# Batch normalisation on one core: a short transfer before every store, and loads issued after 4000 columns

## The chip, the cores and the metric

The kernel runs on one core of a Trainium2 chip. The time is the device time of one execution in microseconds (us); the time before is the median of three runs. Beside it there is one profiled execution with its trace, from which all durations are taken. Engines are named as in the profile: DVE is VectorE, ACT is ScalarE, SP is SyncE; the DMA engines are the sixteen that move data between memory (HBM) and the on-chip buffers (SBUF) for this core.

## The reference

An inference batch normalisation of a 32 x 256 x 128 x 128 float32 tensor, with one mean, variance, factor and offset per channel:

```python
def reference(x, gamma, beta, running_mean, running_var):
    eps = 1e-5
    mean = running_mean.reshape(1, -1, 1, 1)
    ...
    return gamma * (x - mean) / np.sqrt(var + eps) + beta
```

The kernel computes it as `x * scale + shift`, with `scale = gamma / sqrt(var + eps)` and `shift = beta - mean * scale` for each channel. The tensor is 536.87 MB; it is read once and written once.

## The kernel before

**Tiles.** `xr` and `outr` view the tensor as 64 tiles (NT): 32 images by two blocks of 128 channels. A tile has 128 partitions (channels) of 16,384 columns, that is 128 rows of 65,536 bytes, 8.39 MB. Three buffers `bufs[0..2]` hold one tile each; tile i uses buffer i mod 3, is computed in place and stored from there. [...]

**Head** (lines 90 to 128). SP issues the left half of tile 0, then four loads of parameters (L93), each of which puts the same 1024 bytes into 16 rows, then the right half (L97) and tiles 1 and 2 (L99). VectorE and ScalarE turn the parameters into `scale_t` and `shift_t`.

**VectorE** (L155 to L158) takes the left columns of each tile in two instructions at L132: columns 0 to VFIRST (2560), which counts the semaphore `vfirst`, then VFIRST to VMOST (14,336), which counts `vdone`. The last tile goes to VLAST (9216), the first to VHEAD (8192) in one instruction.

**ScalarE** (L166 to L173) takes the other columns with one activation at L143 (2048 columns of most tiles), which counts `adone`, waits for `vdone`, and issues the store of the tile (L171) on its own queue. Before the activation, for tiles 1 to 61, it waits at L168 for `gone(i - 1)`: all of the store of the tile before has been written. So at most one store is in flight for most of the run.

**SP** (L161 to L164) issues the load of tile i when the store of tile i - 3, which used the same buffer, is gone, and when `vfirst` has reached i - 1: VectorE has done the first 2560 columns of tile i - 1, so that tile has landed. So at most one load is in flight too after the head. At the end SP waits for the last three stores (L177).

A DMA of a whole tile gives each of the sixteen DMA engines eight rows of 65,536 bytes and, behind them, a packet of 4 bytes that counts the semaphore. Loads issued by SP are on queue q1, stores issued by ScalarE on queue q10; each DMA engine serves both.

Of the kernel before, what the change touches and what calls it, by code (L numbers as in the profile page):

```python
# [8 lines left out]
NBUF = 3  # L9
PAD = 936  # L10
NHEAD = 3
VFIRST = 2560
VMOST = 14336
VHEAD = 8192
VLAST = 9216


@with_exitstack
def kernel(
    ctx: ExitStack,  # L20
    tc: tile.TileContext,
    x: bass.AP,
    gamma: bass.AP,
    beta: bass.AP,
    running_mean: bass.AP,
    running_var: bass.AP,
    out: bass.AP,
):
    nc = tc.nc
    eps = 1e-5  # L30
    f32 = mybir.dt.float32

    N, C, H, W = x.shape
    P = nc.NUM_PARTITIONS
    assert C % P == 0
    NCB = C // P
    HW = H * W
    NT = N * NCB
    B = 32
    NQ = P // B  # L40
    NE = 16
    NPAR = 4

    xr = x.rearrange("n (cb p) h w -> (n cb) p (h w)", p=P)
    outr = out.rearrange("n (cb p) h w -> (n cb) p (h w)", p=P)

    params = ctx.enter_context(tc.tile_pool(name="params", bufs=1))
    data = ctx.enter_context(tc.tile_pool(name="data", bufs=1))
    params.tile([P, PAD], f32, name="pad", tag="pad")
    bufs = [data.tile([P, HW], f32, name=f"t{s}", tag=f"t{s}") for s in range(NBUF)]  # L50
    rows = params.tile([B, NPAR * C], f32, name="rows", tag="rows")
    turned = params.tile([B, NPAR * C], f32, name="turned", tag="turned")
    par = params.tile([P, NPAR, NCB], f32, name="par", tag="par")
    eps_t = params.tile([P, 1], f32, name="eps_t", tag="eps")
    std_t = params.tile([P, NCB], f32, name="std_t", tag="std")
    rstd_t = params.tile([P, NCB], f32, name="rstd_t", tag="rstd")
    scale_t = params.tile([P, NCB], f32, name="scale_t", tag="scale")
    ms_t = params.tile([P, NCB], f32, name="ms_t", tag="ms")
    shift_t = params.tile([P, NCB], f32, name="shift_t", tag="shift")

    loaded = [tc.alloc_semaphore(f"loaded{s}") for s in range(NBUF)]
    stored = [tc.alloc_semaphore(f"stored{s}") for s in range(NBUF)]
    early = tc.alloc_semaphore("early")
    first = [tc.alloc_semaphore(f"first{s}") for s in range(NHEAD)]
    vfirst = tc.alloc_semaphore("vfirst")
    vdone = tc.alloc_semaphore("vdone")
    adone = tc.alloc_semaphore("adone")
    fetched = tc.alloc_semaphore("fetched")  # L70
    vec = tc.alloc_semaphore("vec")
    act = tc.alloc_semaphore("act")

    with tc.tile_critical():  # L74
        count = [0]

        def step(inst, sem=None, value=None):
            if sem is not None:
                inst._wait_ge(sem, value)
            elif count[0]:  # L80
                inst._wait_ge(vec, count[0])
            inst.then_inc(vec, 1)
            count[0] += 1
            return count[0]

        left, right = slice(0, HW // 2), slice(HW // 2, HW)
        last = NT - 1


        nc.sync.dma_start(out=bufs[0][:, left], in_=xr[0][:, left]).then_inc(early, 16)  # L90
        zeroed = step(nc.vector.memset(rows[:], 0.0))  # L91
        for r, ap in enumerate((running_var, gamma, beta, running_mean)):
            inst = nc.sync.dma_start(out=rows[0:NE, r * C : (r + 1) * C], in_=ap.partition_broadcast(NE))  # L93
            if r == 0:
                inst._wait_ge(vec, zeroed)
            inst.then_inc(fetched, 16)
        nc.sync.dma_start(out=bufs[0][:, right], in_=xr[0][:, right]).then_inc(first[0], 16)  # L97
        for i in range(1, NHEAD):
            nc.sync.dma_start(out=bufs[i][:], in_=xr[i]).then_inc(first[i], 16)  # L99

        def landed(i):
            if i < NHEAD:
                return first[i], 16
            s = i % NBUF
            before = 1 if s < NHEAD else 0
            return loaded[s], 16 * (i // NBUF + 1 - before)


        step(nc.vector.memset(eps_t[:], eps))  # L109
        step(nc.vector.transpose(out=turned[:], in_=rows[:]), fetched, 16 * NPAR)  # L110
        blocks = turned.rearrange("p (rc q b) -> p rc q b", q=NQ, b=B)
        flat = par.rearrange("p r cb -> p (r cb)")
        for q in range(NQ):
            placed = step(nc.vector.tensor_copy(out=flat[q * B : (q + 1) * B], in_=blocks[:, :, q, 0]))  # L114
        var_t, gamma_t, beta_t, mean_t = (par[:, r] for r in range(NPAR))
        nc.scalar.activation(  # L116
            out=std_t[:],
            in_=var_t,
            func=mybir.ActivationFunctionType.Sqrt,
            bias=eps_t[:],  # L120
            scale=1.0,
        )._wait_ge(vec, placed).then_inc(act, 1)
        step(nc.vector.reciprocal(out=rstd_t[:], in_=std_t[:]), act, 1)  # L123
        step(nc.vector.tensor_mul(out=scale_t[:], in0=gamma_t, in1=rstd_t[:]))  # L124
        step(nc.vector.tensor_mul(out=ms_t[:], in0=mean_t, in1=scale_t[:]))  # L125
        ready = step(nc.vector.tensor_sub(out=shift_t[:], in0=beta_t, in1=ms_t[:]))  # L126
        nc.vector.wait_ge(vec, ready)
        nc.scalar.wait_ge(vec, ready)

        def vector_part(i, first_col, end):  # L130
            t, cb = bufs[i % NBUF], i % NCB
            return nc.vector.tensor_scalar(  # L132
                out=t[:, first_col:end],
                in0=t[:, first_col:end],
                scalar1=scale_t[:, cb : cb + 1],
                scalar2=shift_t[:, cb : cb + 1],
                op0=mybir.AluOpType.mult,
                op1=mybir.AluOpType.add,
            )

        def scalar_part(i, first_col):
            t, cb = bufs[i % NBUF], i % NCB
            return nc.scalar.activation(  # L143
                out=t[:, first_col:],
                in_=t[:, first_col:],
                func=mybir.ActivationFunctionType.Identity,
                bias=shift_t[:, cb : cb + 1],
                scale=scale_t[:, cb : cb + 1],
            ).then_inc(adone, 1)

        def gone(i):
            return stored[i % NBUF], 16 * (i // NBUF + 1)


        vector_part(0, 0, VHEAD)._wait_ge(early, 16).then_inc(vdone, 1)  # L155
        for i in range(1, NT):
            vector_part(i, 0, VFIRST)._wait_ge(*landed(i)).then_inc(vfirst, 1)
            vector_part(i, VFIRST, VLAST if i == last else VMOST).then_inc(vdone, 1)  # L158


        for i in range(NHEAD, NT):  # L161
            s = i % NBUF
            nc.sync.wait_ge(*gone(i - NBUF))
            nc.sync.dma_start(out=bufs[s][:], in_=xr[i])._wait_ge(vfirst, i - 1).then_inc(loaded[s], 16)  # L164

        for i in range(NT):  # L166
            if 0 < i < NT - 2:
                nc.scalar.wait_ge(*gone(i - 1))  # L168
            scalar_part(i, VHEAD if i == 0 else VLAST if i == last else VMOST)._wait_ge(*landed(i))
            nc.scalar.wait_ge(vdone, i + 1)  # L170
            nc.scalar.dma_start(out=outr[i], in_=bufs[i % NBUF][:])._wait_ge(adone, i + 1).then_inc(  # L171
                stored[i % NBUF], 16
            )  # L173


        for i in range(NT - NBUF, NT):
            nc.sync.wait_ge(*gone(i))  # L177

# [29 lines left out]
```

## Time and profile before

| | us |
|---|---|
| time, median of 3 runs | 2486.29 (2485.91 to 2487.04) |
| the profiled execution, its own time | 2487.21 |
| its span, first to last instruction | 2485.4 |
| VectorE busy | 505.3 (20%) |
| ScalarE busy | 144.9 (6%) |
| load, issue to landing, median | 37.0 |
| store, issue to landing, median | 36.5 |

How to read the profile: the span is what one execution took from its first to its last instruction; the time of the execution holds a little more. The page gives the busy share of each engine and of the DMA engines in 40 equal slices, the DMA queues with the share of the sixteen engines' span that their packets took, the chain of work that ended last, followed back from the end, and groups of instructions with their mean duration. A timeline line has start and length in us, engine, line of the code, operation, and in brackets how long the engine stood idle before it and what released it; a length that covers several instructions ("x2") runs from the first's start to the last's end. The trace also holds a record of each DMA packet: queue, bytes, start and duration.

VectorE waited for landing loads for 1938.7 us in total, ScalarE for stores to be gone for 2243.3 us, SP for stores for 1693.3 us and for VectorE's first columns for 689.5 us.

### The profile page before, as it was taken

The page shows a single profiled execution, that of the slowest core. Times are in us where ns is not written, and L with a number is a line of the kernel's source. Part 1 is how long each engine was busy: PE and PEld are TensorE (multiplying, and loading weights), DVE is VectorE, ACT ScalarE, POOL GpSimd, SP SyncE. Part 2 cuts the span into 40 slices and gives each one's busy share as a digit, 9 for nine tenths or more (in the row PEclk, how much of TensorE's full clock was granted, in tenths as well). Part 3 has the DMA queues.
Part 4 walks back from the last instruction along what each step waited for, and adds up shares of the span by engine and source line. Part 5 has one row for each costly group of instructions (what it writes and reads, how often), then busy time and mean ns, then how long its engine had stood idle before and what let it go on. Part 6 is the DMA issues. An engine that isn't in the chain of part 4 may idle for free.

```text
span 2485.4 us, 578 instructions
## 1 busy us (share of the span) xinstructions
DVE 505.3 (20%) x138; ACT 144.9 (6%) x66; POOL 0.2 (0%) x4
## 2 busy tenths in 40 slices
DVE  2122121221212212122121121211212212122120
ACT  1000000000000000000000000000000000000001
POOL 0000000000000000000000000000000000000000
DMA  9999999999999999999999999999999999999999
GB/s 421 424 439 438 422 439 433 428 438 436 426 438 437 425 438 437 428 436 436 437 427 437 436 427 438 431 429 439 423 438 437 433 429 436 437 428 437 435 428 405
DMA packets 18708, 1073.85 MB, mean 432 GB/s; under 512 B 2128, under 2 KB 2192, under 8 KB 2192
## 3 DMA queue, kind: packets, MB, share of 16 engines
q1 hardware_dynamic: 9488, 536.94, 50.0%
q10 hardware_dynamic: 9216, 536.88, 49.9%
q14 instruction: 4, 0.03, 0.0%
HBM read 536.94 MB, written 536.87 MB: 432 GB/s over the span
## 4 chain that ended last, share of the span: by engine, by line
DMA 93%; DVE 4%; another core or an unknown queue 1%; ACT 0%; issue 0%; SPq 0%; DVEq 0%
DMA t<-in_x_dram 93%; DVE t L132 4%; ACT t L143 0%; SPq L93 0%; DVE rows L91 0%; SPq L97 0%; DVE eps_t L109 0%; DVEq L203 0%; SPq L74 0%
## 5 line engine op out<-in xcount | busy, mean ns | idle before, releaser
L132 DVE TENSOR_SCALAR t<-t,scale_t,shift_t 128x11776 f32<-128x11776 f32 (+2 forms) x127 | 501.8, 3993 | 1938.8 <-DMA t<-in_x_dram 1938.7
L143 ACT ACTIVATE t<-t,shift_t,scale_t 128x2048 f32<-128x2048 f32 (+1 forms) x64 | 143.3, 2239 | 2299.2 <-DMA out_dram<-t 2243.3
L110 DVE STREAM_TRANSPOSE turned<-rows 32x1024 f32<-32x1024 f32 x1 | 1.2, 1232 | 12.0 <-DMA rows<-in_running_mean_dram 12.0
L116 ACT ACT_TABLE_LOAD x1 | 1.3, 1283 | 0.9 <-SPq L74 0.9
L91 DVE MEMSET rows<- 32x1024 f32 x1 | 0.9, 912 | 1.2 <-SPq L74 1.2
L116 ACT ACTIVATE std_t<-par,eps_t 128x2 f32<-128x2 f32 x1 | 0.3, 295 | 14.1 <-DVE par L114 14.1
L114 DVE COPY par<-turned 32x8 f32<-32x8 f32 x4 | 0.6, 162 | 0.1
L123 DVE RECIPROCAL rstd_t<-std_t 128x2 f32<-128x2 f32 x1 | 0.2, 165 | 0.4 <-ACT std_t L116 0.4
L125 DVE TENSOR_TENSOR ms_t<-par,scale_t 128x2 f32<-128x2 f32 x1 | 0.2, 161 | 0.0
L126 DVE TENSOR_TENSOR shift_t<-par,ms_t 128x2 f32<-128x2 f32 x1 | 0.2, 161 | 0.0
L124 DVE TENSOR_TENSOR scale_t<-par,rstd_t 128x2 f32<-128x2 f32 x1 | 0.2, 160 | 0.0
L192 POOL MEMSET const-bfloat16-1.0<- 128x1 bf16 x1 | 0.1, 101 | 0.0
L192 POOL MEMSET const-uint8-127<- 128x1 uint8 x1 | 0.1, 101 | 0.0
L192 POOL MEMSET const-float32-0.0<- 128x1 f32 x1 | 0.1, 98 | 0.2 <-issue 0.2
L192 POOL MEMSET const-float32-1.0<- 128x1 f32 x1 | 0.1, 98 | 0.0
L109 DVE MEMSET eps_t<- 128x1 f32 x1 | 0.1, 59 | 0.1
## 6 DMA issues: line engine op xcount, KB each, us to landing
t<-in_x_dram SPq DMA_DIRECT2D x2, 4096.0 KB, 15.9
out_dram<-t ACTq DMA_DIRECT2D x64, 36.5
t<-in_x_dram SPq DMA_DIRECT2D x63, 37.0
rows<-in_running_var_dram SPq DMA_DIRECT2D x1, 16.0 KB, 11.2
rows<-in_gamma_dram SPq DMA_DIRECT2D x1, 16.0 KB, 11.1
rows<-in_beta_dram SPq DMA_DIRECT2D x1, 16.0 KB, 10.8
rows<-in_running_mean_dram SPq DMA_DIRECT2D x1, 16.0 KB, 10.7
```

The costliest lines, as they stand in the source:

```text
L91: zeroed = step(nc.vector.memset(rows[:], 0.0))
L109: step(nc.vector.memset(eps_t[:], eps))
L110: step(nc.vector.transpose(out=turned[:], in_=rows[:]), fetched, 16 * NPAR)
L114: placed = step(nc.vector.tensor_copy(out=flat[q * B : (q + 1) * B], in_=blocks[:, :, q, 0]))
L116: nc.scalar.activation(out=std_t[:], in_=var_t, func=mybir.ActivationFunctionType.Sqrt, bias=eps_t[:], scale=1.0,)._wait_ge(vec, placed).t ...
L123: step(nc.vector.reciprocal(out=rstd_t[:], in_=std_t[:]), act, 1)
L124: step(nc.vector.tensor_mul(out=scale_t[:], in0=gamma_t, in1=rstd_t[:]))
L125: step(nc.vector.tensor_mul(out=ms_t[:], in0=mean_t, in1=scale_t[:]))
L126: ready = step(nc.vector.tensor_sub(out=shift_t[:], in0=beta_t, in1=ms_t[:]))
L132: return nc.vector.tensor_scalar(out=t[:, first_col:end], in0=t[:, first_col:end], scalar1=scale_t[:, cb : cb + 1], scalar2=shift_t[:, cb ...
L143: return nc.scalar.activation(out=t[:, first_col:], in_=t[:, first_col:], func=mybir.ActivationFunctionType.Identity, bias=shift_t[:, cb : ...
L192: nc = _bacc.Bacc("TRN2", target_bir_lowering=False, num_devices=1)
```

## The change

For tiles 1 to 61 ScalarE's part becomes two activations: 640 columns (STEP), which count a new semaphore `begun`, and the remaining 2048, which count `adone` as before. Between them it issues a small transfer of its own queue: eight rows (HALF) of 16 float32, 64 bytes each, all from the first 16 values of `gamma` into the first 16 columns of eight partitions of `pad`, which nothing reads. Its issue waits for `begun`, so for the end of the 640 columns, and, from tile 2 on, for the small transfer of the tile before (`aside`). Then come the 2048 columns, the wait for `vdone`, and the store. VMOST goes from 14,336 to 13,696, so that VectorE gives up the 640 columns, and VFIRST from 2560 to 4000: the load that waits for `vfirst` waits for 4000 columns of VectorE. At the end SP waits for the last small transfer too.

```diff
-VFIRST = 2560
-VMOST = 14336
+VFIRST = 4000
+VMOST = 13696
+STEP = 640
+HALF = 8
...
-        def scalar_part(i, first_col):
+        def scalar_part(i, first_col, end, done):
             t, cb = bufs[i % NBUF], i % NCB
             return nc.scalar.activation(
-                out=t[:, first_col:],
-                in_=t[:, first_col:],
+                out=t[:, first_col:end],
+                in_=t[:, first_col:end],
...
-            ).then_inc(adone, 1)
+            ).then_inc(done, 1)
...
         for i in range(NT):
+            first_col = VHEAD if i == 0 else VLAST if i == last else VMOST
             if 0 < i < NT - 2:
                 nc.scalar.wait_ge(*gone(i - 1))
-            scalar_part(i, VHEAD if i == 0 else VLAST if i == last else VMOST)._wait_ge(*landed(i))
+                scalar_part(i, first_col, first_col + STEP, begun)._wait_ge(*landed(i))
+                first_col += STEP
+                if i > 1:
+                    nc.scalar.wait_ge(aside, 16 * (i - 1))
+                nc.scalar.dma_start(
+                    out=pad[0:HALF, 0:16], in_=gamma[0:16].partition_broadcast(HALF)
+                )._wait_ge(begun, i).then_inc(aside, 16)
+            scalar_part(i, first_col, HW, adone)._wait_ge(*landed(i))
             nc.scalar.wait_ge(vdone, i + 1)
             nc.scalar.dma_start(out=outr[i], in_=bufs[i % NBUF][:])._wait_ge(adone, i + 1).then_inc(
                 stored[i % NBUF], 16
             )
 
 
+        nc.sync.wait_ge(aside, 16 * (NT - 3))
         for i in range(NT - NBUF, NT):
             nc.sync.wait_ge(*gone(i))
```

## The prediction

> **What bounds the kernel now.** I read the page's slices of the span and its queues first, then its chain, then the chain in order of time and the timeline of a middle stretch, then the groups by shape.
>
> ```profile
> DMA  9999999999999999999999999999999999999999
> q1 hardware_dynamic: 9488, 536.94, 50.0%
> q10 hardware_dynamic: 9216, 536.88, 49.9%
> DMA 93%; DVE 4%; another core or an unknown queue 1%; ACT 0%; issue 0%; SPq 0%; DVEq 0%
> ```
>
> The sixteen DMA engines have work in every slice; the packets of the load queue (q1) and the store queue (q10) fill 99.9% of sixteen engines' span. The chain says "93% loads", but that is not where time could be won: while a load is on the chain the engines also carry the store.
>
> ```profile
> 435.99 36.96 DMA t<-in_x_dram
> 472.95 0.02 issue
> 472.98 1.62 DVE t L132
> 474.60 0.02 issue
> 474.62 36.97 DMA t<-in_x_dram
> ...
> 400.00:2400.00 2000.00, 408.34 (x103) 107.23 (x52) 0.00 (x0) 1.00 1.00 433
> ```
>
> Columns above: start and length in us of a piece of the chain; the last line is a window of 2000 us (busy DVE, ACT, POOL, clock, DMA share, GB/s). One tile takes 474.62 - 435.99 = 38.63 us. A tile is 128 rows of 65,536 bytes in and as many out, so each engine has 8 + 8 rows to move: 38.63 / 16 = 2.414 us a row. The trace's packet records say the same directly: of 16,256 packets of 65,536 bytes, loads and stores alike, about 98% took 2418 ns (the next starts 4 ns before the end), and none under 2410. That holds whether the other engines are loading or storing at that moment. So an engine has its own rate and no idle time: the 1032 data packets of an engine (16 of them half as long) are 2471.9 us; the first starts 2.0 us into the span and the last ends 1.7 us before its end; what is over is 9.8 us on the last engine, 3.7 (loads) and 2.4 (stores) of it, on the mean of the engines, by packets that took longer. **The whole gain to be had is 9.8 us (0.4%); any nanosecond added to the packets of an engine that is behind is added to the time.**
>
> Why no engine runs dry is the second thing to read:
>
> ```profile
> 657.35 2.09 ACT L143 ACTIVATE t<-t,shift_t,scale_t 128x2048 f32<-128x2048 f32 x1 [37.32 <-DMA out_dram<-t]
> 659.47 0.34 ACTq L171 DMA_DIRECT2D out_dram<-t  x1
> 666.98 7.93 DVE L132 TENSOR_SCALAR t<-t,scale_t,shift_t 128x2560 f32<-128x2560 f32 x2 [31.50 <-DMA t<-in_x_dram]
> 668.62 0.33 SPq L164 DMA_DIRECT2D t<-in_x_dram  x1
> 695.96 2.09 ACT L143 ACTIVATE t<-t,shift_t,scale_t 128x2048 f32<-128x2048 f32 x1 [36.52 <-DMA out_dram<-t]
> 698.08 0.34 ACTq L171 DMA_DIRECT2D out_dram<-t  x1
> ```
>
> One load and one store are in flight. A load's end releases VectorE, and 1.64 us later the next load is issued; a store's end releases ScalarE, and 2.12 us later the next store is issued. By the packet records an engine's cycle is: four store rows alone (the load is being turned round), four pairs, four load rows alone (the store is being turned round). Four rows are 9.66 us of cover for each turnaround.
>
> **The change part by part.** Durations come from the groups by shape:
>
> ```profile
> L132 DVE TENSOR_SCALAR t<-t,scale_t,shift_t 128x11776 f32<-128x11776 f32 x62 | 397.2, 6407 | 0.0
> L143 ACT ACTIVATE t<-t,shift_t,scale_t 128x2048 f32<-128x2048 f32 x62 | 129.8, 2093 | 2250.8 <-DMA out_dram<-t 2243.3 <-DMA t<-in_x_dram 7.5
> L132 DVE TENSOR_SCALAR t<-t,scale_t,shift_t 128x2560 f32<-128x2560 f32 x63 | 101.6, 1612 | 1938.7 <-DMA t<-in_x_dram 1938.7
> L143 ACT ACTIVATE t<-t,shift_t,scale_t 128x7168 f32<-128x7168 f32 x1 | 6.4, 6361 | 41.5 <-DMA t<-in_x_dram 41.5
> ```
>
> 1. Loads follow 4000 columns. VectorE: (6407 - 1612) / (11776 - 2560) = 0.520 ns a column, so 1612 + 1440 x 0.520 = 2361 ns: the load is issued 0.75 us later. Its second piece has 9696 columns, about 5.3 us; the store waits for it, but VectorE ends some 21 us before ScalarE starts that tile (666.98 + 7.93 against 695.96). The load's first packets start 3.4 to 5.2 us after issue while stores run, and four more store rows stand behind them, so nothing runs dry: some engines do a fifth store row alone. Cost 0; without that cover 61 x 0.75 = 46 us.
>
> 2. ScalarE's part is 2688 columns in two instructions, and a DMA issue between. Slope (6361 - 2093) / (7168 - 2048) = 0.834 ns a column, so 640 columns take 2093 - 1408 x 0.834 = 0.92 us; the issue 0.34 (the row at L171), steps between 0.03 to 0.05. The store is issued about 1.35 us later (0.92 + 0.34 + 0.09). Behind it on ScalarE nothing waits but the next tile. On the engine that is furthest behind the first store packet of line 659.47 starts 4.58 us after issue, as its loads last that long; 3.23 us would be left. From issue to a first packet takes 1.01 us on an idle engine (the span's first load, issued at 0.95) and at most 2.42 us (the smallest seen here without a gap). So that engine stays fed, with 0.8 to 2.2 us to spare. Engines ahead may stand still up to about 1 us and then are less ahead, which costs nothing at the end. Cost 0; without that cover 61 x 1.35 = 82 us.
>
> 3. The wait for the short transfer before (`aside`) was satisfied a tile earlier, the last wait on SP lies under the last stores: 0. No queue of POOL is passed. The added ScalarE instructions, transfers and waits make the program about 40% longer; there were four fetches of 8192 bytes on q14 in mid-run, two more at 0.4 to 0.7 us on one engine each: 0.5 us taken.
>
> 4. **The short rows themselves.** 61 transfers of 8 rows of 64 bytes, each a packet and a 4-byte count on one engine, between two long packets. This isn't in the trace. Nearest rows from both sides: below, a 4-byte packet takes 9 ns and shifts the next by 6, a row of 1024 bytes takes 46; so 0.016 us and, were it to smooth what follows, less than nothing (a rival below). Above, a short packet lets too little be fetched behind it: after the four q14 packets of 8192 bytes (309 ns) the next 65,536 bytes took 2528, 2542, 2569 and 2768 ns, that is 110, 124, 151 and 350 too many; the three small ones are those with a 4-byte packet between. And the four 16-row parameter loads in the head, one row per engine each:
>
> ```profile
> 10.00:12.00 2.00, 0.00 (x0) 0.00 (x0) 0.00 (x0) 1.00 0.99 426
> 12.00:13.00 1.00, 0.00 (x0) 0.00 (x0) 0.00 (x0) 1.00 1.39 455
> 13.00:14.00 1.00, 0.00 (x0) 0.00 (x0) 0.00 (x0) 1.00 0.58 234
> 14.00:16.00 2.00, 1.67 (x4) 0.00 (x0) 0.00 (x0) 1.00 1.10 475
> 16.00:18.00 2.00, 1.39 (x7) 0.29 (x1) 0.00 (x0) 1.00 1.06 459
> 18.00:20.00 2.00, 2.00 (x1) 0.00 (x0) 0.00 (x0) 1.00 0.80 344
> ```
>
> These ten us moved 409 GB/s on the mean, against 433 in mid-run: 0.54 us lost, 0.14 a row. The packet records agree: mostly 0.48 us from the last long packet's end to where the next would have begun, and that next took about 1500 ns where 1213 is usual. I take the mean of the three q14 rows, 0.128, and 0.016 for the packets: 0.144 us a tile, as a single foreign packet amid long ones is nearest to it. 61 x 0.144 = 8.8 us on eight engines, which nothing hides as they are never idle. The ends kept for the range are 0 and 0.66 us (309 - 4 + 350, if the whole slot of the slowest q14 case is a fetch delay that 8192 bytes only covered): 0 to 40 us.
>
> [...]
>
> **Sum.** 8.8 + 0.5 = 9.3 us. The profiled execution took 2487.21 us, 1.8 more than its span of 2485.4, and is 0.9 over the median of 2486.29. The median plus 9.3 is 2495.6.
>
> **The rivals.**
> - *The short row is nearly free* (0.016 to 0.06 us): 1 to 4 us, 2487 to 2490, no change that can be told; a measurement of this kernel tells 0.2%, 5 us, from none. For it: counts between long packets shift them by 6 ns, so what is fetched ahead reaches past a tiny packet. Against it: q14 and the head. Not slower; it decides if the fetch ahead spans two packets. 0.33.
> - *The whole delay is paid*: 0.45 to 0.66 us a tile, 2514 to 2527. For it: both q14 and the head come to 0.43 to 0.66 us for a slot of any size. Against: in the head rows followed each other at 48 ns. 0.08.
> - *The engines run dry at each store.* If the store gets in after the slowest engine's loads have ended, the load's count is not held back by a store packet; the next load then comes after three store rows (0.37 + 2.36 + 0.05 + about 3.5 = 6.3 us, under 7.24), so only three load rows cover the store: 2.41 + 0.54 + 3.48 + (1.01 to 2.42) - 7.24 = 0.2 to 1.6 us idle per tile, which keeps itself up. 12 to 98 us, 2498 to 2584. Against it: with four rows, where the kernel is now, 0.8 us or more is left. 0.08.
> - *Faster.* The slower packets cluster where the first packets of a transfer meet the other queue: by position in the cycle (slots of 2.414 us after a load's issue) 25 and 15 ns a packet in slots 2 and 4, and 37 in slot 13, the store's start. If the short row and the new offsets took all of that away, 61 x 0.077 = 4.7 us less 1: about 2483; with all 6.1 us of long packets gone, 2480. Against: nothing ties them to who goes first. 0.07, about 0.05 of it beyond 0.2%.
>
> **How the numbers follow.** Forecast (0.11 to 0.36 us a tile): 0.44, own range 2492 to 2509, at 2495.6. The range takes in the free row and half of the faster case below and the lower part of the two slow rivals above: 2483 to 2517, which leaves out 0.05 below and some 0.13 above. Slower by over 0.2%: 0.44 + 0.08 + 0.08 = 0.60 less what of them stays under; same 0.35; faster 0.05.
>
> **What would show it.** Right: a load-to-load period of about 38.8 us, packets of 65,536 bytes just behind the 64-byte ones at 2.5 to 2.6 us, on eight engines, and idle time on the others. Wrong: a period of 38.65 and 2418 ns behind the short rows (free); a DMA share clearly under 1 in mid-run on all engines, with gaps before the first store packets (dry). The load should be issued about 2.4 us after VectorE starts and the store 3.5 us after ScalarE does. The forecast fails if the fetch ahead isn't disturbed by a 64-byte packet.

## The result and the profile after

The changed kernel takes 2636.68 us (median of 4 runs, 2635.94 to 2640.04) where the kernel before took 2486.33 us beside it: 1.0609 times the time, 95% interval 1.0593 to 1.0625. The prediction was 2495.6 us with a range from 2483 to 2517. Where a kernel's executions lie further apart than 1.5%, its ratio here and below goes by the faster ones, while the time given is the median of all. The profiled execution has a span of 2634.3 us against 2485.4, 148.9 us more, or 2.44 us for each of the 61 tiles that are changed.

The page of the changed kernel, the lines that answer to those shown of before:

```profile
span 2634.3 us, 761 instructions
DMA  9999999999999999999999999999999999999999
q1 hardware_dynamic: 9488, 536.94, 49.8%
q10 hardware_dynamic: 10192, 536.91, 48.8%
DMA 92%; DVE 6%; another core or an unknown queue 1%; ACT 0%; issue 0%; SPq 0%; DVEq 0%
```

The shares still say "full": 98.6% against 99.9%. That is 1.3% of the span, 34 us, of engines that stand idle; the other 115 us do not show as idle time at all. They are in packets that take longer. Here the share says that packets are open, not that bytes move as fast as before: the window from 400 to 2400 us has a share of 0.99 and moved 407 GB/s, against 1.00 and 433 before.

The chain in order of time (start, length, what) and three windows (length, busy DVE, ACT, POOL, clock, DMA share, GB/s) of the changed kernel:

```profile
453.32 38.93 DMA t<-in_x_dram
492.25 0.02 issue
492.27 2.37 DVE t L136
494.64 0.02 issue
494.66 38.63 DMA t<-in_x_dram
...
400.00:2400.00 2000.00, 372.51 (x98) 147.58 (x98) 0.00 (x0) 1.00 0.99 407
696.90:697.60 0.70, 0.00 (x0) 0.00 (x0) 0.00 (x0) 1.00 0.02 1
738.00:738.80 0.80, 0.00 (x0) 0.00 (x0) 0.00 (x0) 1.00 0.01 0
```

A tile takes 494.66 - 453.32 = 41.34 us there, about 41.2 over the run, against 38.63. The two short windows are the moment before a store. A window counts a packet where it starts, so a share of 0.02 says that next to none starts there. The timeline of one tile around the first of them:

```profile
693.36 0.92 ACT L147 ACTIVATE t<-t,shift_t,scale_t 128x640 f32<-128x640 f32 x1 [37.85 <-DMA out_dram<-t]
694.31 0.31 ACTq L178 DMA_DIRECT2D pad<-in_gamma_dram  x1
694.67 2.09 ACT L147 ACTIVATE t<-t,shift_t,scale_t 128x2048 f32<-128x2048 f32 x1 [0.39 <-ACT t L147]
696.79 0.36 ACTq L183 DMA_DIRECT2D out_dram<-t  x1
698.13 7.60 DVE L136 TENSOR_SCALAR t<-t,scale_t,shift_t 128x4000 f32<-128x4000 f32 x2 [33.60 <-DMA t<-in_x_dram]
700.52 0.33 SPq L168 DMA_DIRECT2D t<-in_x_dram  x1
```

The store is issued 3.43 us after ScalarE starts, the load 2.39 us after VectorE does; both were forecast to 0.1 us. But by the packet records the engines' last load rows end from 696.80 to 697.78, and the first store rows start from 697.66 to 697.80: the store's rows come about 0.9 us after its issue, when the loads of all engines but two are over, and fourteen of the sixteen engines have run dry, for up to 1.0 us. From there the records go on as follows, the same in nearly every tile: three store rows alone (four before), the first two at 2430 to 2460 ns, the third mostly at 2.8 to 3.5 us, then the first load row at 2.8 to 4.6 us, and from there 2418 ns again until three load rows are left alone, and most of the engines run dry once more. On the mean of the engines the run has 120.4 us of packet time over 2418 ns a row and 33.4 us of gaps before store rows: 1.97 and 0.55 us a tile.

### The profile page after: what moved, and what is told of

The parts are those of the page before. It is cut to its first block, busy times and chain, and to the rows that moved or that the text cites. A ratio compares the mean times of both kernels' runs of the same rounds, so it can differ in the third digit from the quotient of the medians.

```text
span 2634.3 us, 761 instructions
## 1 busy us (share of the span) xinstructions
DVE 484.7 (18%) x138; ACT 201.5 (8%) x127; POOL 0.2 (0%) x4
## 4 chain that ended last, share of the span: by engine, by line
DMA 92%; DVE 6%; another core or an unknown queue 1%; ACT 0%; issue 0%; SPq 0%; DVEq 0%
DMA t<-in_x_dram 92%; DVE t L136 6%; ACT t L147 0%; SPq L97 0%; DVE rows L95 0%; SPq L101 0%; DVE eps_t L113 0%; DVEq L216 0%; SPq L78 0%
## 5 line engine op out<-in xcount | busy, mean ns | idle before, releaser
L136 DVE TENSOR_SCALAR t<-t,scale_t,shift_t 128x9696 f32<-128x9696 f32 (+2 forms) x127 | 481.2, 3830 | 2105.5 <-DMA t<-in_x_dram 2105.4
L147 ACT ACTIVATE t<-t,shift_t,scale_t 128x2048 f32<-128x2048 f32 (+2 forms) x125 | 199.9, 1599 | 2388.7 <-DMA out_dram<-t 2313.2
```

Of the source, the lines that this page charges most:

```text
L136: return nc.vector.tensor_scalar(out=t[:, first_col:end], in0=t[:, first_col:end], scalar1=scale_t[:, cb : cb + 1], scalar2=shift_t[:, cb ...
L147: return nc.scalar.activation(out=t[:, first_col:end], in_=t[:, first_col:end], func=mybir.ActivationFunctionType.Identity, bias=shift_t[: ...
```

## The experiments

The labels of the runs are those of the quoted expectations. All ratios are to the kernel before on the same chip, with the 95% interval.

### Which of the three edits

The change makes loads later, stores later, and puts short rows ahead of each store. Each was tried without the others or left out.

**v_only**: loads later alone.

```diff
-VFIRST = 2560
+VFIRST = 4000
```

> The kernel before with VFIRST = 4000 alone: the load is issued 0.75 us later, nothing else is changed. My theory: the changed kernel is slow because the store is issued 1.35 us later, so that the engines' loads end before the store is there; they stand idle, then all start the store within 0.2 us of each other and disturb one another. By it this kernel keeps four store rows alone before the load and four load rows alone before the store, and takes 2485 to 2489 us. Rival 'late load': the later load is what breaks the cycle; then it is slow, 2550 to 2640 us.

Measured: 2486.91 us, ratio 1.0004 (0.9994 to 1.0013). The later load costs nothing. It does change the cycle, though not as I expected: by the packet records six store rows run alone for most of the run in place of four, and so six load rows alone.

**delay_only**: the store later alone, by more columns for ScalarE.

```diff
-VMOST = 14336
+VMOST = 12716
```

> The kernel before with VMOST = 12716: ScalarE takes 3668 columns in one instruction (about 3.45 us), so the store is issued about as late as in the changed kernel (3.5 us after the store before is gone), with no short rows and with loads after 2560 columns. 'Late store' theory: three store rows alone, idle engines before each store, packets over 2418 ns at the switch, a period near 41.2 us, 2600 to 2640 us. Rival 'short rows': the 64-byte rows disturb the engines; without them 2485 to 2490 us.

Measured: 2638.01 us, ratio 1.0614 (1.0598 to 1.063). Without any short row the whole loss is there. Its timeline:

```profile
694.02 3.44 ACT L143 ACTIVATE t<-t,shift_t,scale_t 128x3668 f32<-128x3668 f32 x1 [37.87 <-DMA out_dram<-t]
697.49 0.34 ACTq L171 DMA_DIRECT2D out_dram<-t  x1
698.76 7.09 DVE L132 TENSOR_SCALAR t<-t,scale_t,shift_t 128x2560 f32<-128x2560 f32 x2 [34.19 <-DMA t<-in_x_dram]
```

The load lands 1.3 us after the store's issue, as in the changed kernel; in the kernel before it landed 7.5 us after it (659.47 to 666.98).

**rows_early**: the changed kernel with its short rows and later loads, but ScalarE's pieces made short so that the store should be in time.

```diff
-VMOST = 13696
+VMOST = 15296
```

> The changed kernel with VMOST = 15296: ScalarE's pieces are 640 and 448 columns, so the store is issued about 2.1 us after the store before is gone, as in the kernel before, with the short rows in front of it and loads after 4000 columns. 'Late store' theory: no idle engines, a period of 38.65 to 38.8 us, 2485 to 2497 us, and what is over 2486 is the short rows' own price (0.144 us a tile in my prediction would give 2495). Rival 'short rows': stays above 2550 us.

Measured: 2620.74 us, ratio 1.0539 (1.05 to 1.0579). So the short rows are enough as well, and my theory of the lateness alone was too narrow. The timeline shows one thing that comes with them:

```profile
691.44 0.31 ACTq L178 DMA_DIRECT2D pad<-in_gamma_dram  x1
691.80 0.76 ACT L147 ACTIVATE t<-t,shift_t,scale_t 128x448 f32<-128x448 f32 x1 [0.39 <-ACT t L147]
692.59 1.79 ACTq L183 DMA_DIRECT2D out_dram<-t  x1
```

The store's issue takes 1.79 us (median of the run 1.58) in place of 0.34. By the packet records the first of the short rows is taken up at 694.04, when the first engine has ended its loads, and the store's issue ends 0.34 us later, at 694.38. In most of the tiles with such a long issue the first store row starts about 0.51 us after the issue's end, so the long issue does make the store late. What holds the issue up isn't shown: no engine had taken its short row when the store's issue began, in any of the 61 tiles, yet 12 of the 61 issues took 0.34 us.

**after_v2560**: the changed kernel with the loads early again.

```diff
-VFIRST = 4000
+VFIRST = 2560
```

> The changed kernel with VFIRST back at 2560: short rows and late store, loads 0.75 us earlier. 'Late store' theory: an earlier load doesn't help, the load still comes after three store rows; 2600 to 2640 us. Rival 'late load': back to 2485 to 2495 us.

Measured: 2638.82 us, ratio 1.0618 (1.0602 to 1.0633). A load 0.75 us later or earlier makes no difference here.

**late_v4000**: the changed kernel's late store and later loads, no short rows (`VFIRST = 4000`, `VMOST = 12716` in the kernel before).

> The late store of delay_only (VMOST = 12716, one ScalarE instruction of 3668 columns) together with loads after 4000 columns, no short rows. With VFIRST = 4000 alone the loads came so late that six store rows and then six load rows run alone, 14.5 us of cover in place of 9.7. Theory A, 'cover': the late store fits under it, 2485 to 2490 us, and so the changed kernel, which is this one with short rows, is slow by its short rows: they are taken up only when the loads have ended, and the store behind them with them. Theory B, 'late store alone': slow as delay_only, 2620 to 2640 us.

Measured: 2637.62 us, ratio 1.0603 (1.0586 to 1.0621). Theory A fell: by the packet records three store rows run alone, and the cover of six rows that v_only showed is not there when the store is late from the start. Taking the short rows away doesn't mend the change.

**rows_first**: the short rows first thing, with the store only 0.35 us late.

```diff
...
             if 0 < i < NT - 2:
                 nc.scalar.wait_ge(*gone(i - 1))
+                if i > 1:
+                    nc.scalar.wait_ge(aside, 16 * (i - 1))
+                nc.scalar.dma_start(
+                    out=pad[0:8, 0:16], in_=gamma[0:16].partition_broadcast(8)
+                ).then_inc(aside, 16)
...
```

> The kernel before with the short transfer issued first thing after the store before is gone, ahead of one ScalarE instruction of 2048 columns; the store is issued about 0.35 us later than before, loads after 2560 columns. Theory A: here the short rows are taken up between load rows, two packets before the loads end, so the store is not held back: 2486 to 2497 us, and what is over 2486 is the rows' own price. Rival 'any short row ahead of a store starves the engines': 2600 to 2640 us.

Measured: 2621.12 us (2581.46 to 2635.91), ratio 1.0451 (1.0371 to 1.053). Theory A fell here too. Either of the two edits, the late store or the short rows ahead of it, is enough to lose 4.5% or more. The store's issue was rarely held up here (median 0.34 us), so what rows_early showed is not needed; how the short rows tip the cycle in this run was not followed further.

### What holds the cycle up

The packet records show what both edits touch. In the kernel before, at the tile of line 659.47, fourteen engines end their last load row and that load's 4-byte count comes next (661.88 to 662.47). On the other two a store row comes next (663.13 and 664.05), and the count stands behind it, 2.41 us later (665.55 and 666.46). From 80 us on VectorE starts 0.30 to 0.58 us after the load's last count, in the kernel before and in the changed one. In the four kernels of the table, the records let nearly every load end be matched with its count by time (from 76 us on, without the last load). Here they are by the time at which the last load row started, counted from the store's issue:

| last load row started, us after the store's issue | before: count held / all | changed: held / all | late_v7200: held / all | after_v7200: held / all |
|---|---|---|---|---|
| under 0.75, or before the issue | 0 / 385 | 0 / 974 | 0 / 4 | 0 / 804 |
| 0.75 to 1.25 | 123 / 324 | none | 239 / 295 | 0 / 171 |
| over 1.25 | 260 / 264 | none | 630 / 633 | none |

So in the kernel before and in late_v7200 a store row came ahead of the count if the store's issue was about 1.0 us old when an engine started its last load row, that is 1.0 + 2.41 = 3.4 us before its loads ended. One count decides for the tile, the one that comes last: it stood behind a store row in all 62 loads that VectorE waited for after 80 us in the kernel before, in v_only, in late_06 and in late_v7200, and in one or two of 62 in the changed kernel, delay_only and after_v7200. In the kernel before the engine that ends last had 4.58 us in the tile of line 659.47: 1.2 us to spare, and its count was held. In the changed kernel no count in the table is held. The first tile shows the fall; here the kernel before, then the changed one:

```profile
76.89 0.34 ACTq L171 DMA_DIRECT2D out_dram<-t  x1
84.36 7.93 DVE L132 TENSOR_SCALAR t<-t,scale_t,shift_t 128x2560 f32<-128x2560 f32 x2 [23.65 <-DMA t<-in_x_dram]
```

```profile
78.39 0.37 ACTq L183 DMA_DIRECT2D out_dram<-t  x1
82.12 7.60 DVE L136 TENSOR_SCALAR t<-t,scale_t,shift_t 128x4000 f32<-128x4000 f32 x2 [21.62 <-DMA t<-in_x_dram]
```

The store is issued 1.50 us later, and the load lands 2.24 us earlier, about one row. The next load is then issued earlier (84.51 against 86.00) and is taken up after three store rows; so only three load rows are left alone at the end, 7.24 us in place of 9.66, and the next store is again too late. The state kept itself up: one of 62 counts that VectorE waited for was held in the changed kernel, against 62 of 62. This makes a test: the load held back by other means must mend it, whatever the store does.

**late_v7200**: the late store of delay_only, with loads after 7200 columns (`VFIRST = 7200`, `VMOST = 12716` in the kernel before).

> The late store of delay_only (3668 ScalarE columns, no short rows) with VFIRST = 7200, so that the load is issued 2.4 us later than there. Theory 'held count': in the kernel before, a load's 4-byte count on the engine that ends last stands behind a store row (2.41 us), as the store is seen about 1.0 us after its issue, before that engine's last load row starts. If the store is seen later, the count comes at once, the next load comes after three store rows in place of four, and then only three load rows cover the store: the engines run dry and the state keeps itself up. A load held back by 2.4 us by other means must restore four rows and four rows: 2484 to 2492 us. Rival 'late store alone': an engine that waits for a later store is slow whatever the load does: 2600 to 2640 us.

Measured: 2486.20 us, ratio 1.0005 (0.9995 to 1.0015), against 2638.01 with `VFIRST = 2560` and 2637.62 with 4000. One of its ten executions took 2651.96 us, so the fast cycle can still be lost. The timeline has the store issued 3.47 us after the store before is gone, as in the slow kernels, and the load lands 8.6 us behind it:

```profile
692.76 3.44 ACT L143 ACTIVATE t<-t,shift_t,scale_t 128x3668 f32<-128x3668 f32 x1 [35.24 <-DMA out_dram<-t]
696.23 0.34 ACTq L171 DMA_DIRECT2D out_dram<-t  x1
704.79 7.09 DVE L132 TENSOR_SCALAR t<-t,scale_t,shift_t 128x7200 f32<-128x7200 f32 x2 [31.55 <-DMA t<-in_x_dram]
```

Five, later six store rows run alone. So a store 1.35 us later need not cost anything; what costs is the earlier load that it brings about.

**after_v7200**: the changed kernel with `VFIRST = 7200`.

> The changed kernel with VFIRST = 7200 in place of 4000, short rows as they are. Theory 'held count': four store rows alone again, 2486 to 2500 us; what is over late_v7200 is the price of the short rows themselves (8.8 us in the prediction). Rival 'short rows starve the engines': 2600 us or more.

Measured: 2516.16 us (2487.08 to 2522.31), ratio 1.0101 (1.004 to 1.0161); 120 us of the 150 are mended by one constant. Four store rows alone are back, though no count is held (last column of the table, also where the kernel before held 123 of 324). So in these runs it is the time of the next load that matters, whatever sets it. That a short row stands where the store row would is an argument, not shown. The profiled execution (2522.31) is 35 us over that of late_v7200, and most of it is store rows that come late to their turn: the store packets have 26.2 us over 2418 ns on the mean of the engines, against 0.1 in late_v7200. One of the four executions took 2487.08 us, so even this isn't lost each time.

**late_06** and **late_10**: doses of the late store in the kernel before (`VMOST = 13616` and `VMOST = 13136`).

> The kernel before with 2768 ScalarE columns in one instruction: the store comes 0.60 us later, no short rows, loads after 2560 columns. Theory 'held count': on the engine that ends last the store was seen some 1.2 us before it had to be, so 0.6 us change nothing: 2484 to 2490 us. Rival 'every ns counts': 2500 us or more.

Measured: 2509.02 us, ratio 1.0095 (1.008 to 1.011). Neither theory: the cycle keeps its four rows (a period near 39.1 us), but 23.7 us of store packets over 2418 ns, 2.4 before, go with engines whose loads end early, whose first store row takes up to 3.5 us with no gap before it. What makes that row longer isn't shown. So there is a second, gradual cost of a later store, below the edge.

> The same with 3248 columns: the store comes 1.00 us later. Theory 'held count': at the edge; either as before (2484 to 2490 us) or, once a slower packet has tipped it, slow for the rest of the run, anywhere between 2490 and 2640 us, and never between the two in a single tile. Rival 'gradual': about 1.0 us a tile, 2545 us.

Measured: four executions of 2514.83, 2644.39, 2648.79 and 2742.60 us. The chain in order of time of the profiled one (the 2742.60) shows the steps:

```profile
125.68 37.85 DMA t<-in_x_dram
...
165.20 37.42 DMA t<-in_x_dram
...
321.48 39.38 DMA t<-in_x_dram
...
362.53 39.43 DMA t<-in_x_dram
...
2095.12 41.85 DMA t<-in_x_dram
...
2138.63 41.81 DMA t<-in_x_dram
```

Loads start 39.5 us apart (125.68 to 165.20) with four store rows alone, 41.1 apart (321.48 to 362.53) with three, and 43.5 apart (2095.12 to 2138.63) with two. It fell to three rows at the fifth changed tile and to two at the ninth, and never climbed back. The cycle has states, and within one execution the same code ran in three of them. A delay of 1.00 us was enough to fall, by the times in three of the four executions.

### The short rows' own price

**rows_sp**: the short rows on the load queue, behind each load, where no store stands behind them.

```diff
...
             nc.sync.dma_start(out=bufs[s][:], in_=xr[i])._wait_ge(vfirst, i - 1).then_inc(loaded[s], 16)
+            if i > NHEAD:
+                nc.sync.wait_ge(aside, 16 * (i - NHEAD))
+            nc.sync.dma_start(
+                out=pad[0:8, 0:16], in_=gamma[0:16].partition_broadcast(8)
+            ).then_inc(aside, 16)
...
```

> The kernel before with the same short rows (8 rows of 64 bytes) issued by SP right behind each load, on the load queue, where they stand in front of no store; 61 of them on eight engines. It measures the term that my prediction rested on, the rows' own price: at 0.144 us a tile 2495 us, at 0.66 us 2526 us. By the long packets that directly follow a 64-byte row between two load rows in after_v7200 (no ns too many in the median of 24) it is about 0.02 us a tile: 2485 to 2489 us.

Measured: 2486.05 us, ratio 1.0002 (0.9993 to 1.0011). Each of the 488 packets of 64 bytes took 11 ns, and the long packet behind it, where the records show which it is (484 of them), about 1 ns too many on the mean.

### The long packets at the switch

Two thirds of the loss and more, 1.97 of 2.52 us a tile, are packets of up to 4.6 us where stores and loads meet. Sorted over eleven kernels, the two of the change among them, by how many engines start the store within 0.2 us of each other, tiles with three store rows alone lose, after the first store row, 1.95 us an engine on the mean where 14 to 16 engines start together (280 tiles), 0.62 where 8 to 10 do (21 tiles), and 0.34 with 7 or fewer (25 tiles); with four rows alone 1.69 us (17 tiles) against 0.04 and 0.02 (85 and 68). It is not a clean rule: nine tiles of rows_first with 8 to 10 engines together lost 1.0 to 1.9 us. Engines that have run dry start close together, in the tile above from 697.66 to 697.80. My guess was that engines in lockstep collide. Three pairs of runs were to show it by setting half of the engines off against the other half.

**four_short** and **four_long**: the changed kernel with four short transfers in place of one; the diff is that of four_short, and four_long has the columns 0:PAD on both sides.

```diff
...
-                nc.scalar.dma_start(
-                    out=pad[0:HALF, 0:16], in_=gamma[0:16].partition_broadcast(HALF)
-                )._wait_ge(begun, i).then_inc(aside, 16)
+                nc.scalar.wait_ge(begun, i)
+                for j in range(4):
+                    nc.scalar.dma_start(
+                        out=pad[8 * j : 8 * j + HALF, 0:16], in_=xr[0][8 * j : 8 * j + HALF, 0:16]
+                    ).then_inc(aside, 16)
...
```

> The changed kernel with four short transfers (8 rows of 64 bytes from x) where it has one; the control for the next run. The store comes about 1 us later still. Engines idle, then start together: 2640 to 2720 us, with the same slow packets at the switch to loads.

> As the run before, but the rows have 3744 bytes: each of the four holds eight engines for about 0.14 us, so half of the engines start the store some 0.5 us after the other half. Theory 'lockstep': the 2 us lost per tile at the switch come from sixteen engines within 0.2 us of each other; here they shrink by half or more, 40 to 120 us less than four_short. Rival 'the switch itself is slow after three store rows': as four_short, or up to 40 us more for the longer rows.

Measured, one execution each: 2727.59 and 2760.18 us. Not the saving that lockstep was to give, but also not the comparison that was meant: both fell within four tiles to a cycle with no store row alone, where loads run dry in place of stores.

**stag_half** and **stag_all**: delay_only with a transfer before the store that holds eight engines, or all, for 0.6 us (an estimate: 16,384 bytes a row, at 2418 ns for 65,536); it writes rows of the last tile's output, which the last store writes again. ROWS is 8 in stag_half and 16 in stag_all.

```diff
...
             nc.scalar.wait_ge(vdone, i + 1)
+            if 0 < i < NT - 2:
+                if i > 1:
+                    nc.scalar.wait_ge(aside, 16 * (i - 1))
+                nc.scalar.dma_start(
+                    out=outr[last][0:ROWS, 0:4096], in_=bufs[i % NBUF][0:ROWS, 0:4096]
+                )._wait_ge(adone, i + 1).then_inc(aside, 16)
+            if i == last:
+                nc.scalar.wait_ge(aside, 16 * (NT - 3))
...
```

> delay_only (late store, engines dry before each store, 41.2 us a tile, 2638 us) with one more transfer right before each store on its queue: 8 rows of 16,384 bytes of the tile, which hold eight of the sixteen engines for about 0.6 us (they go to the last tile's output, which is overwritten at the end). So eight engines start the store 0.6 us after the others. Theory 'lockstep': sixteen engines that start within 0.2 us of each other collide at the switch from stores to loads, 2 us a tile; two groups 0.6 us apart collide less: at least 0.7 us a tile faster than stag_all. Rival 'the switch itself': no more than 0.2 us a tile (12 us) from stag_all.

> The control: 16 rows of 16,384 bytes, one on each engine, so all sixteen start the store 0.6 us later and still together. Theory 'lockstep': 41.2 + 0.6 and 0.2 to 0.4 for the issue, about 42.2 us a tile, 2690 to 2710 us. Rival: stag_half comes out the same.

Measured: 2749.49 us (1.1062, 1.1042 to 1.1083) and 2781.69 us (1.1192, 1.1172 to 1.1213), 32 us apart, between the two marks, and again after a fall to no store row alone, so they don't decide either.

**stag2_half** and **stag2_all**: the same with `VMOST = 13184` and `VFIRST = 4800`.

> stag_half with 3200 ScalarE columns in place of 3668, which takes back the extra issue, so that the store comes about 3.5 us after the store before is gone as in the changed kernel, and with loads after 4800 columns, so that three store rows alone are kept and the cycle doesn't slide on to two and to none as it did in stag_half and stag_all. Eight engines start the store 0.3 us or more after the other eight. Theory 'lockstep': at most 1.3 us a tile of packets over 2418 ns at the switch, against 2.0 in the changed kernel, and at least 0.7 us a tile less than stag2_all. Rival 'the switch itself': the same 2 us in both.

> The control: sixteen rows of 16,384 bytes, one on each engine, all engines together. About 41.4 us a tile, 2650 us, with 2 us a tile of packets over 2418 ns at the switch by both theories.

Measured: 2825.83 us (2787.50 to 2864.17) and 2820.22 us (2810.12 to 2830.32), no difference that can be told, and no fair comparison: stag2_half settled with two store rows alone and its stores run dry, stag2_all mostly with one and its loads run dry. In its profiled execution (2864.17) stag2_half kept two groups of eight engines 2.4 us apart at the store's start and still lost 1.8 us a tile in long packets. So sixteen engines in lockstep are not needed for the loss. The first group started within 0.1 us and lost 2.3 us a tile, the second was spread over 0.8 us and lost 1.4, which is the way that lockstep would have it, but the groups differ in more than that. What makes these packets long stays open: they go mostly with engines that start together after running dry, but no run here took the one away and kept the other.

### Does the kernel before already pay?

**early_09**: `VMOST = 15360` in the kernel before, 1024 columns for ScalarE.

> The kernel before with 1024 ScalarE columns in place of 2048: the store is issued 0.85 us earlier. If the kernel before loses 2.4 us (the store packets over 2418 ns, mean of the engines) because a store is at times seen too late to be fetched ahead, this saves most of them: 2482 to 2486 us. Rival: these packets have another cause, no change.

Measured: 2487.47 us, ratio 1.0007 (0.9998 to 1.0016). Store packets over 2418 ns fell from 2.4 to 0.5 us on the mean of the engines, but the time did not. No version of these beats the kernel before.

## Why the prediction was wrong

- **The bound** was read rightly: an engine has 2418 ns a row, nothing to gain beyond 9.8 us, and what was added to the engines' packets and gaps was added to the time. 1.97 + 0.55 us a tile is 154 us on the mean of the engines, less the 6 us that the kernel before had in long packets: 148 of the span's 148.9.
- **Part 1, later loads at cost 0**: right as put (v_only, 1.0004), and the issue came 2.39 us after VectorE's start as worked out. The rival price of 46 us if the cover were gone played no part.
- **Part 2, the store 1.35 us later at cost 0: this is the step that failed.** It counted four load rows as fixed cover, and took 3.23 us from issue to the first store packet as enough because 1.01 to 2.42 were seen to be enough. But the four rows were themselves a result of the store being early: by the table it had to be issued about 1.0 us before the last load row started, 3.4 us before the loads ended, to hold the load's count. There were 1.2 us to spare in that tile and not 0.8 to 2.2 beyond the delay; 1.35 went over it, and in late_10 1.00 was enough. delay_only shows the loss with this part alone (2638.01 us), late_v7200 shows it gone with this part in place (2486.20). Even under the edge zero was not right: late_06, 0.60 us later, cost 23 us.
- **Part 3, two more fetches, 0.5 us**: one more came (five packets of 8192 bytes on q14 in place of four); no run prices it; by the prediction's estimate, 0.4 to 0.7 us, it is too small to matter here.
- **Part 4, the short rows at 0.144 us a tile**: mis-sized; rows_sp gives no measurable price (ratio 1.0002). The rows from which it came (an 8192-byte fetch, four rows in the head) were near in size but not in effect. No run shows a fetch ahead, from which the sum and its rival argued; what the runs show is the 65,536 bytes behind a short packet, 110 to 350 ns too many after the four q14 packets of before, about 1 ns in rows_sp. That short rows ahead of a store could make it late and tip the cycle was not in the sum; rows_early and rows_first show that this alone costs 4.5 to 5.4%.
- **The rival of the dry engines** (0.08) had the mechanism: three store rows, then three load rows, kept up by itself. It was turned down for the reason of part 2, and put the deciding point at the end of the loads, one row and 1.0 us too late. Its price, 0.2 to 1.6 us a tile, has the gaps in it (0.55 measured) but not the long packets (1.97), so that even it ended at 2584.
- **What would show it**: the prediction named gaps before the first store packets as a sign of the dry state, and these came; the DMA share on which it also counted went only from 1.00 to 0.99.

## What to carry to other kernels

Where two transfer streams take turns, as loads and stores do here, the cover of one can be made by the timing of the other (four rows, 9.66 us, became three, 7.24): before calling a delay covered, work out the cycle that follows with the cover one packet smaller, and see whether it comes back. Here a store 1.50 us later moved a load's landing 2.24 us earlier, about a packet, so a delay of 1.35 us was priced neither at 0 nor at 1.35, and a later load mended the late store (late_v7200, 2486.20 us against 2638.01). A nearly full DMA share didn't prove a full rate (0.99 at 407 GB/s, 1.00 at 433): compare GB/s in a window, and the packets' own durations.

## What the runs showed of the hardware

- In the kernel before, a store row came right behind an engine's last load row if the store was issued about 1.0 us before that row started (0 of 385 under 0.75 us, 123 of 324 from 0.75 to 1.25, 260 of 264 over 1.25); the packet that counts the load then came a row (2.41 us) later, else at once.
- In rows_early the issue of a store took 1.58 us (median) in place of 0.34, about 1.15 us after the issue of a short transfer on the same queue; 12 of 61 took 0.34 all the same, and the cause is not settled.
- The first row of a store took up to 3.5 us in place of 2.42 with no gap before it (late_06); the cause is not shown.
- Where fourteen to sixteen engines started a store within 0.2 us of each other, after three store rows alone (280 tiles), they lost 1.95 us an engine on the mean at the switch to loads, in packets of up to 4.6 us; the cause is not settled.
